# A transformer block in split fp32 on one core: how a VectorE-fed stream starts its products, seven weight tiles side by side

## The chip, the cores and the metric

The kernel runs on one core of a Trainium2 chip. TensorE multiplies (PE in the profile), VectorE (DVE) and ScalarE (ACT) do elementwise work, GpSimd (POOL) some adds and a few DMA issues, SyncE (SP) issues the weight loads. The metric is the device time of one execution in microseconds (us), the median over runs. A measurement of this kernel can tell about 1% from no change, some 22 us.

## What is computed

One block on 272 tokens (16 meta tokens and 256 real ones) of width 2048: half an FFN, a mixer, half an FFN, each between two RMS norms:

```python
h = h + 0.5 * _rmsnorm(_swiglu(_rmsnorm(h, norm_ffn1_pre), ffn1_w_gu, ffn1_w_down), norm_ffn1_post)
m = _hybrid_mixer(_rmsnorm(h, norm_mix_pre), w_in, ..., w_out, cos, sin)
h = h + _rmsnorm(m, norm_mix_post)
h = h + 0.5 * _rmsnorm(_swiglu(_rmsnorm(h, norm_ffn2_pre), ffn2_w_gu, ffn2_w_down), norm_ffn2_post)
return h[:, N_META:]
```

The FFN is `(silu(h @ W_g) * (h @ W_u)) @ W_down` with inner width 5632. The mixer multiplies by `w_in`, runs a multi-scale pooling and a latent attention of 16 heads, gates both, adds them and multiplies by `w_out`. All is fp32.

## The kernel before

**Layout.** Activations lie transposed: 128 partitions by tokens, so the width of 2048 is 16 tiles of the stream (`KD = 16`), each 128 x 272, or 128 x 256 from the mixer's gates on, where the meta tokens are no longer needed. `T` is that width: `L = 272` or `R = 256`. `h` is the residual stream, `h[:, k]` its tile k.

**Split products.** An fp32 product is made of three products of rounded parts, high by high, high by low, low by high (`mm3`, L221 to L225). At width 256 the first two are one matmul of 512 columns into the two halves of a PSUM bank (`mm_wide`, L227 to L231), and `join` adds the halves when the bank is read. Every operand therefore has a high part (a rounded copy) and a low part (the difference).

**Weights.** All weight tiles (128 x 128) stand in DRAM in the order of use, eight to a DMA. Class `Weights` cuts each load into pieces of four tiles (`PT = 4`): ScalarE writes a piece's high part (L93), VectorE subtracts it to make the low part (L102). There are six buffers for pieces (`HL = 6`). `take`, called before each weight tile's matmuls, loads and divides ahead: when piece p is taken, the high parts up to piece p + 4 and the low parts up to p + 3 are queued. Every engine works through its queue in the order in which the program issues it; there is no scheduler that reorders.

**Steps that come later.** `later` keeps a list of small steps with a delay in weight tiles; `take` counts one tick per tile and issues the steps that are due. The reading of banks, the activation and the splitting of results go through it, so that they sit between the weight pieces in the engines' queues.

**The stream.** A stage that begins with a norm doesn't wait for it: the factor of the norm is one number per token, so the products use the unscaled stream times the gain, and the results are scaled by `rs` when they are read. Class `Stream` (L290 to L319) makes the 16 tiles of x one by one. `step(s)` for tile k = s + 1 queues, in this order: the high part of tile k on ScalarE (L304), the update of tile k + 1 (below), the low part of tile k on VectorE (L308), and its square (ScalarE, L280) with the add into `acc` (GpSimd, L283). The update, made in `advance` (L378), finishes the stage before: `t[k] * b` on VectorE (L382; b is the norm's factor, read from PSUM), then the add into `h[k]` (L383), on VectorE for tiles 0 and 1 and on GpSimd for the other 14. After the last tile `scale` sums the squares over partitions on TensorE (`rms_sums`), takes root and reciprocal, and `spread` broadcasts the factor on TensorE (`rms_spread`, L264) and copies it to `rs` on VectorE (L318).

**The wave.** In `products` (L321) a stage with a stream first runs six results side by side, each in a PSUM bank: for each k the stream's step, then one weight tile for each of the six results. The sums come ahead of the products of the last k, the spread behind them. The six banks are read afterwards, one every 12 ticks (`SPACE`). All other results follow one by one over all k, in banks called `m`. There are eight PSUM banks.

**The transition.** `post` (L358) ends a stage: it reads each result, squares it, scales it into `t`, sums the squares (`rms`, L267), with `WARM = (3, 7)` idle matmuls of 128 columns ahead of the spread and behind it. There are three waves with a stream: the first FFN's, whose stream arrives from DRAM (`arrive`), the mixer's first products (transition T1) and the second FFN's (transition T2). The end of the kernel (L776 to L788) multiplies `t` by the last norm's factor, adds `h` and writes the result, on VectorE from b in PSUM and for four of the 16 tiles on GpSimd from a copy in `rs`.

## Time and profile before

| | |
|---|---|
| median of 3 runs | 2237.63 us (2224.92 to 2239.29) |
| the profiled execution | 2238.56 us |
| its span | 2236.8 us |
| PE busy | 2211.0 us, 99% |
| VectorE busy | 1372.7 us, 61% |
| ScalarE busy | 1162.4 us, 52% |
| GpSimd busy | 213.8 us, 10% |
| T1, last down product to the first tile after the wave | 805.09 to 851.98 us |
| T2, the same | 1463.95 to 1508.32 us |
| last norm's factor to the end of the span | 2223.6 to 2236.8 us |

In the lines of the profile L102 is line 102 of the kernel. A group's line has the engine, the operation, output<-input by the program's names, shapes, the count after an x, then the busy time and the mean of one in ns, then the engine's idle time before it and what ended it. A line of the timeline begins with its start from the span's start and its duration, in us; brackets give the idle time before it. A line of the waits has total us, number of times, and the longest. A line of windows has, for each engine, the busy time and the count, then the granted clock, the DMA share and GB/s. Matmuls overlap, so a start-to-start time says what one costs, and a "busy" TensorE may still wait inside.

### The profile page before, as it was taken

The page shows a single profiled execution, that of the slowest core. Times are in us where ns is not written, and L with a number is a line of the kernel's source. Part 1 is how long each engine was busy: PE and PEld are TensorE (multiplying, and loading weights), DVE is VectorE, ACT ScalarE, POOL GpSimd, SP SyncE. Part 2 cuts the span into 40 slices and gives each one's busy share as a digit, 9 for nine tenths or more (in the row PEclk, how much of TensorE's full clock was granted, in tenths as well). Part 3 has the DMA queues.
Part 4 walks back from the last instruction along what each step waited for, and adds up shares of the span by engine and source line. Part 5 has one row for each costly group of instructions (what it writes and reads, how often), then busy time and mean ns, then how long its engine had stood idle before and what let it go on. Part 6 is the DMA issues. An engine that isn't in the chain of part 4 may idle for free.

```text
span 2236.8 us, 39512 instructions
## 1 busy us (share of the span) xinstructions
PE 2211.0 (99%) x15040; PEld 2059.2 (92%) x15040; DVE 1372.7 (61%) x2525; ACT 1162.4 (52%) x2310; POOL 213.8 (10%) x228
## 2 busy tenths in 40 slices
PE   9999999999999999999999999999999999999997
PEld 9999999999999999988899988888888888888886
DVE  6555555555444477766688876587666666655554
ACT  6444444444444454555566655665555555555453
POOL 2000000000000043300132111150000000000001
PEclk9999999999999999999999999999999999999999
DMA  6555555555555545556533355545555555555553
GB/s 232 177 172 175 176 177 170 178 177 174 181 178 169 180 150 171 179 180 196 178 125 133 129 189 191 187 144 192 186 187 185 185 188 188 188 189 180 190 185 124
DMA packets 109311, 393.46 MB, mean 176 GB/s; under 512 B 12288, under 2 KB 13696, under 8 KB 109120
## 3 DMA queue, kind: packets, MB, share of 16 engines
q1 hardware_dynamic: 108576, 389.19, 53.7%
q8 instruction: 118, 1.93, 0.4%
q0 software_dynamic: 400, 1.61, 0.2%
q14 instruction: 73, 0.60, 0.1%
q10 hardware_dynamic: 144, 0.13, 0.0%
HBM read 388.78 MB, written 2.10 MB: 175 GB/s over the span
## 4 chain that ended last, share of the span: by engine, by line
PE 95%; DVE 3%; issue 1%; ACT 0%; DMA 0%; SPq 0%; DVEq 0%; ACTq 0%
PE m L229 30%; PE m L231 15%; PE m L223 13%; PE m L225 13%; PE m L224 13%; DVE lo L102 2%; PE w L229 1%; PE s L665 1%; PE w L231 1%; DVE x L308 1%; PE po L225 1%; PE po L224 1%; PE po L223 1%; PE w L225 1%; PE w L224 1%
## 5 line engine op out<-in xcount | busy, mean ns | idle before, releaser
L102 DVE TENSOR_TENSOR lo<-raw,hi 128x512 fp32r<-128x512 f32 x1472 | 1016.3, 718 | 279.0 <-ACT hi L93 275.2
L93 ACT ACTIVATE hi<-raw 128x512 fp32r<-128x512 f32 x1472 | 894.7, 627 | 448.6 <-PE m L224 279.2
L229 PE MATMUL m<-x,hi 128*128 128x512 f32 x1824 | 643.3, 398 | 0.0
L231 PE MATMUL m<-x,lo 128*128 128x256 f32 x1824 | 512.7, 281 | 0.0
L223 PE MATMUL m<-x,hi 128*128 128x272 f32 (+1 forms) x1488 | 429.4, 289 | 0.0
L225 PE MATMUL m<-x,lo 128*128 128x272 f32 (+1 forms) x1488 | 429.0, 288 | 0.0
L224 PE MATMUL m<-x,hi 128*128 128x272 f32 (+1 forms) x1488 | 428.2, 288 | 0.0
L229 PEld LDWEIGHTS m<-x,hi 128*128 128x128 f32 x1824 | 342.7, 188 | 83.4
L231 PEld LDWEIGHTS m<-x,lo 128*128 128x128 f32 x1824 | 344.6, 189 | 0.0
L224 PEld LDWEIGHTS m<-x,hi 128*128 128x128 f32 x1488 | 282.9, 190 | 0.0
L223 PEld LDWEIGHTS m<-x,hi 128*128 128x128 f32 x1488 | 279.6, 188 | 0.0
L225 PEld LDWEIGHTS m<-x,lo 128*128 128x128 f32 x1488 | 279.5, 188 | 0.0
L283 POOL TENSOR_TENSOR acc<-acc,sq 128x272 f32<-128x272 f32 (+1 forms) x88 | 88.9, 1010 | 1525.7 <-ACT sq L280 1510.5
L229 PE MATMUL m<-a,hi 128*128 128x512 f32 x660 | 233.2, 399 | 0.0
L223 PE MATMUL m<-a,hi 128*128 128x272 f32 (+1 forms) x748 | 215.6, 288 | 0.0
L225 PE MATMUL m<-a,lo 128*128 128x272 f32 (+1 forms) x748 | 215.6, 288 | 0.0
L224 PE MATMUL m<-a,hi 128*128 128x272 f32 (+1 forms) x748 | 215.2, 288 | 0.0
L231 PE MATMUL m<-a,lo 128*128 128x256 f32 x660 | 185.4, 281 | 0.0
L396 DVE TENSOR_TENSOR gu<-m,rs 128x272 f32<-128x272 f32 x82 | 36.2, 442 | 228.5 <-PE m L225 228.5
L229 PEld LDWEIGHTS m<-a,hi 128*128 128x128 f32 x660 | 124.0, 188 | 30.9
L224 PEld LDWEIGHTS m<-a,hi 128*128 128x128 f32 x748 | 142.4, 190 | 0.0
L223 PEld LDWEIGHTS m<-a,hi 128*128 128x128 f32 x748 | 140.7, 188 | 0.0
(214 smaller groups left out, 2723.6 us busy)
## 6 DMA issues: line engine op xcount, KB each, us to landing
raw<-w SPq DMA_DIRECT2D x735, 512.0 KB, 3.6
h<-hT POOLq DMA_DIRECT2D x4, 272.0 KB, 5.4
out<-t SPq DMA_DIRECT2D x8, 128.0 KB, 1.9
out<-t SPq DMA_DIRECT2D x4, 256.0 KB, 2.0
h<-hT SPq DMA_DIRECT2D x1, 544.0 KB, 8.6
raw<-w SPq DMA_DIRECT2D x2, 256.0 KB, 3.5
MA<-tables POOLq DMA_DIRECT2D x1, 480.0 KB, 3.8
h<-hT SPq DMA_DIRECT2D x2, 136.0 KB, 3.5
```

What stands on the lines that cost most here:

```text
L93: nc.scalar.activation(hi, t, AF.Copy)
L102: self.nc.vector.tensor_tensor(lo, t, hi.bitcast(F32), op=ALU.subtract)
L223: mm(o, wh, xh, start=first, stop=False)
L224: mm(o, wh, xl, start=False, stop=False)
L225: mm(o, wl, xh, start=False, stop=last)
L229: mm(b.rearrange("p (b c) -> p b c", b=2), w[0], x.both(k, R), start=first, stop=last, skip_group_check=True)
L231: mm(b[:, :R], w[1], x.hi(k, R), start=False, stop=last, skip_group_check=True)
L283: pool_e.tensor_tensor(acc[:, :T], acc[:, :T], s[:, :T], op=ALU.add)
L308: dve.scalar_tensor_tensor(self.x.lo(k), src, g, hi.bitcast(F32), op0=ALU.mult, op1=ALU.subtract)
L396: scale = lambda src: dve.tensor_tensor(u, src, rs[:, :T], op=ALU.mult)
L665: mm(o, x[:, t], y[:, :n], start=j == 0, stop=j == 4)
```

## The change

1. **The first stream tile of T1 and T2.** In the stage before, three results before its end, ScalarE scales `h[0]` and `t[0]` by the next gain (`old`, `new`). Once the factor b is there, `Stream.begin` makes tile 0 on VectorE alone: `new *= b`, high = `old + new` rounded, `new = old + new`, low = `new` - high. The update of `h[0]` itself, and the squares of tiles 0 and 1, come later, at tile 2.
2. **The order of the first step.** For k = 0 `products.begin` takes all weight tiles and issues for each the two products with the stream's high part; the products with the low part follow for all of them. `Weights.keep` limits the division of pieces meanwhile, so that no buffer still needed is taken.
3. **Seven results side by side** instead of six (`WAVE = 7`) in all three waves. The last of them is read first.
4. **GpSimd's adds in the waves go to VectorE**, those into `h` and those into `acc`, in the first FFN's wave too.
5. **The factor b is copied to SBUF by ScalarE** (`r`), into spare room of `t`'s buffer or, in T1, of the buffer MA, whose allocation and table load move ahead of the first down products. Updates read r, and b's bank is free. At the end of the kernel VectorE and GpSimd both read r.
6. **The sums** come after the third result of the last k, the spread after the sixth.
7. `WARM` is (3, 3).

```diff
-WARM = (3, 7)
-GAP, SPACE = 4, 12
+WARM = (3, 3)
+GAP, SPACE, WAVE = 4, 12, 7
 ...
-        while self.n_split < min(upto, self.total * CH // PT):
+        while self.n_split < min(upto, self.most, self.total * CH // PT):
 ...
+    def keep(self, on):
+        self.most = len(self.order) // PT + HL if on else 1 << 30
 ...
-        pool_e.tensor_tensor(acc[:, :T], acc[:, :T], s[:, :T], op=ALU.add)
+        e.tensor_tensor(acc[:, :T], acc[:, :T], s[:, :T], op=ALU.add)
 ...
+        def begin(self):
+            (old, new, r), hi = self.first, self.x.hi(0)
+            dve.tensor_tensor(new, new, r, op=ALU.mult)
+            dve.tensor_tensor(hi, old, new, op=ALU.add)
+            dve.tensor_tensor(new, old, new, op=ALU.add)
+            dve.tensor_tensor(self.x.lo(0), new, hi.bitcast(F32), op=ALU.subtract)
 
         def step(self, s):
             k, T = s + 1, self.T
+            if k < 0 and self.first:
+                self.begin()
+                return
             todo = self.update(k + 1) if k + 1 < KD else ()
-            if 0 <= k < KD:
+            split = 0 <= k < KD and not (k == 0 and self.first)
+            if split:
                 src, g, hi = h[:, k, L - T :], gain(self.g, k), self.x.hi(k)
                 act(hi, src, AF.Copy, scale=g)
             for f in todo:
                 f()
-            if 0 <= k < KD:
+            if split:
                 dve.scalar_tensor_tensor(self.x.lo(k), src, g, hi.bitcast(F32),
                                          op0=ALU.mult, op1=ALU.subtract)
-                self.last = squares(src, T, k, k == KD - 1)
+            if self.late and k == self.late:
+                for f in self.update(0):
+                    f()
+            if self.late <= k < KD:
+                for j in range(0 if k == self.late else k, k + 1):
+                    self.last = squares(h[:, j, L - T :], T, j, j == KD - 1, dve)
 ...
+        def begin():
+            todo = []
+            W.keep(True)
+            for i in range(wave):
+                w, t = W.take((names[i][0], 0, names[i][1])), T[i] if isinstance(T, list) else T
+                for wi in w:
+                    mm(banks[i][:, :t], wi, x.hi(0, t), start=wi is w[0], stop=False, skip_group_check=wide[i])
+                todo.append((w[0], t))
+            for i, (wh, t) in enumerate(todo):
+                c = R if wide[i] else 0
+                mm(banks[i][:, c : c + t], wh, x.lo(0, t), start=False, stop=False, skip_group_check=wide[i])
+            W.keep(False)
 ...
-                if k == n_k - 1:
-                    spread = stream.scale()
 ...
+            if stream and k == 0:
+                begin()
+                continue
             for i in range(wave):
                 part(i, k, banks[i])
-        if stream:
-            spread()
-        for i in range(wave):
-            later((1 + SPACE * i, lambda i=i: evac(i, banks[i], wide[i])))
+                if stream and k == n_k - 1 and i in (2, 5):
+                    spread = stream.scale() if i == 2 else spread()
+        for j in range(wave):
+            i = (j - 1) % wave if stream else j
+            later((1 + SPACE * j, lambda i=i: evac(i, banks[i], wide[i])))
 ...
+                if j == KD - 3 and g_pre is not None:
+                    for name, src in (("old", h[:, 0, L - T :]), ("new", t[:, 0, :])):
+                        first.append(temp(name)[:, :T])
+                        act(first[-1], src, AF.Copy, scale=gain(g_pre, 0))
 ...
-        return t, rms([acc] + last, T, DM, half, wait)
+        b = rms([acc] + last, T, DM, half, wait)
+        if first:
+            first.append(b[:, :T])
+        act(r, b[:, :T], AF.Copy)
+        return t, r, first
 ...
-            e = pool_e if k > 1 else dve
-            return (lambda: dve.tensor_tensor(t[:, k, :], t[:, k, :], b[:, :T], op=ALU.mult),
-                    lambda: e.tensor_tensor(hk, hk, t[:, k, :], op=ALU.add))
-        return Stream(T, g_pre, update)
+            return (lambda: dve.tensor_tensor(t[:, k, :], t[:, k, :], r, op=ALU.mult),
+                    lambda: dve.tensor_tensor(hk, hk, t[:, k, :], op=ALU.add))
+        return Stream(T, g_pre, update, first)
 ...
-        products(names, KD, x.x, T, 6, evac, x)
+        products(names, KD, x.x, T, WAVE, evac, x)
 ...
-        o, f = t[:, a : a + n, :], (b if e is dve else rs)[:, :R]
+        o = t[:, a : a + n, :]
+        f = r[:, None, :].to_broadcast([P, n, R]) if n > 1 else r[:, None, :]
         e.tensor_tensor(o, o, f, op=ALU.mult)
         e.tensor_tensor(o, o, h[:, a : a + n, NMETA:], op=ALU.add)
         nc.sync.dma_start(out[:, a : a + n, :], o)
-        if a == 0:
-            act(rs[:, :R], b[:, :R], AF.Copy)
```

More of the change, by code (lines that the diff above doesn't have):

```diff
@@ L72, in __init__ @@
         self.n_loaded = self.n_split = self.n_low = 0
+        self.most = 1 << 30
     def load(self, upto):
@@ L272, in rms, with squares @@
         return b
-    def squares(src, T, j, last=False):
+    def squares(src, T, j, last=False, e=pool_e):
         if j == 0:
@@ L290, in build, with __init__ @@
     class Stream:
-        def __init__(self, T, g, update):
-            self.T, self.g, self.update = T, g, update
+        def __init__(self, T, g, update, first=None):
+            self.T, self.g, self.update, self.first = T, g, update, first
             self.x = Two(KD, T, "x")
             self.last = []
+            self.late = 2 if first else 0
+        def begin(self):
[4 more added lines that the diff above has]
+            dve.tensor_tensor(self.x.lo(0), new, hi.bitcast(F32), op=ALU.subtract)
         def step(self, s):
             k, T = s + 1, self.T
+            if k < 0 and self.first:
+                self.begin()
+                return
             todo = self.update(k + 1) if k + 1 < KD else ()
-            if 0 <= k < KD:
+            split = 0 <= k < KD and not (k == 0 and self.first)
+            if split:
                 src, g, hi = h[:, k, L - T :], gain(self.g, k), self.x.hi(k)
@@ L355, in products, with post @@
             evac(i, b, wide[i])
-    def post(names, n_k, x, T, g_post, half, wave, wait):
-        t = slot3(KD, T, F32, "t")
-        last = []
+    def post(names, n_k, x, T, g_post, half, wait, g_pre, wave, spare=None):
+        room = slot(SLOT, F32, "t")
+        t = room[:, : KD * T].rearrange("p (a b) -> p a b", a=KD)
+        r = room[:, KD * T : KD * T + T] if T == R else spare()
+        last, first = [], []
         def evac(j, b, wide):
@@ L409, in evac @@
                   (GAP, lambda: dve.tensor_tensor(lo, u, hi.bitcast(F32), op=ALU.subtract)))
-        products(names, KD, x.x, T, 6, evac, x)
+        products(names, KD, x.x, T, WAVE, evac, x)
         later.flush()
         load_table()
-        return post([(w_down, j) for j in range(KD)], KF, a, T, g_post, True, 0, wait)
+        return post([(w_down, j) for j in range(KD)], KF, a, T, g_post, True, wait, g_pre, 0, spare)
     warm(10, zero)
@@ L423, in arrive, with spare @@
                 lambda: pool_e.dma_start(h[:, k + 4 : k + 6, :], hT[:, k + 4 : k + 6, :]),)
-    t, b = ffn(Stream(L, G_F1PRE, arrive), "ffn1_w_gu", "ffn1_w_down", G_F1POST, WARM)
-    x = advance(t, b, L, G_MPRE)
-    MA = slot(SLOT, F32, "MA")
-    pool_e.dma_start(MA[:, :C_KPE], tables_d)
+    made = {}
+    def spare():
+        made["MA"] = slot(SLOT, F32, "MA")
+        pool_e.dma_start(made["MA"][:, :C_KPE], tables_d)
+        return made["MA"][:, SLOT - L :]
+    after = ffn(Stream(L, G_F1PRE, arrive), "ffn1_w_gu", "ffn1_w_down", G_F1POST, WARM, G_MPRE, spare)
+    x = advance(*after, L, G_MPRE)
+    MA = made["MA"]
     cos, sin, mask = MA[:, C_COS:C_SIN], MA[:, C_SIN:C_MASK], MA[:, C_MASK:C_KPE]
@@ L521, in evac_in @@
             windows(i - 9)
-    products(names, KD, x.x, width, 6, evac_in, x)
+    products(names, KD, x.x, width, WAVE, evac_in, x)
     zp_rest = slot(SLOT, F32, "zp")
@@ L772, in build @@
     load_table()
-    t, b = post([("w_out", m) for m in range(KD)], KD, y, R, G_MPOST, False, 6, WARM)
-    t, b = ffn(advance(t, b, R, G_F2PRE), "ffn2_w_gu", "ffn2_w_down", G_F2POST, (0, 0))
+    after = post([("w_out", m) for m in range(KD)], KD, y, R, G_MPOST, False, WARM, G_F2PRE, 6)
+    t, r, _ = ffn(advance(*after, R, G_F2PRE), "ffn2_w_gu", "ffn2_w_down", G_F2POST, (0, 0), None)
     for a, n, e in ((0, 1, dve), (1, 1, dve), (3, 1, pool_e), (2, 1, dve), (4, 2, dve), (8, 1, pool_e), (6, 2, dve),
                     (9, 2, dve), (11, 1, pool_e), (12, 2, dve), (15, 1, pool_e), (14, 1, dve)):
-        o, f = t[:, a : a + n, :], (b if e is dve else rs)[:, :R]
-        if n > 1:
-            f = f[:, None, :].to_broadcast([P, n, R])
-        else:
-            f = f[:, None, :]
+        o = t[:, a : a + n, :]
+        f = r[:, None, :].to_broadcast([P, n, R]) if n > 1 else r[:, None, :]
         e.tensor_tensor(o, o, f, op=ALU.mult)
```

4 lines of the change are left out of this document (2 added, 2 removed).

## The prediction

> **What bounds the kernel now.** I read the page first, then the waits of the two transitions, then their timelines, then the tail.
>
> ```profile
> span 2236.8 us, 39512 instructions
> PE 2211.0 (99%) x15040; PEld 2059.2 (92%) x15040; DVE 1372.7 (61%) x2525; ACT 1162.4 (52%) x2310; POOL 213.8 (10%) x228
> ```
> ```profile
> 700.00:800.00 100.00, 100.00 (x799) 100.00 (x798) 44.87 (x67) 44.78 (x79) 5.16 (x7) 1.00 0.56 181
> 2100.00:2200.00 100.00, 100.00 (x568) 86.69 (x567) 51.13 (x78) 49.23 (x89) 5.75 (x6) 1.00 0.59 189
> ```
>
> TensorE sets the time. In an undisturbed stretch (second fence, busy time by window) it issues 799 matmuls in 100 us, 0.125 us each: a weight tile at width 272 costs three, 0.376 us. In the narrow half 568 are 284 pairs, 0.352 us per tile. The diff leaves the tile count alone, so it can only win what TensorE loses elsewhere: at the transition into the mixer (T1) and into the second FFN (T2). There one engine holds it:
>
> ```profile
> PE w L224 <- DVE x L308: 2.8, 6, 0.5
> PE w L229 <- DVE x L308: 3.7, 7, 0.7
> ```
>
> TensorE waits for VectorE's low part of the next stream tile, in T1 (L224) and T2 (L229). Why VectorE is late stands in the groups of T1's wave (812 to 846 us) beside the weight differences of a quiet stretch (600 to 700 us, last row):
>
> ```profile
> L102 DVE TENSOR_TENSOR lo<-raw,hi 128x512 fp32r<-128x512 f32 x21 | 25.9, 1259 | 0.0
> L283 POOL TENSOR_TENSOR acc<-acc,sq 128x272 f32<-128x272 f32 x13 | 15.9, 1223 | 0.0
> L383 POOL TENSOR_TENSOR h<-h,t 128x272 f32<-128x272 f32 x13 | 12.6, 967 | 6.8 <-DVE t L382 6.8
> L102 DVE TENSOR_TENSOR lo<-raw,hi 128x512 fp32r<-128x512 f32 x67 | 45.4, 692 | 55.6 <-ACT hi L93 55.6
> ```
>
> The weight difference takes 1.259 us beside GpSimd's adds and 0.692 us without: 21 x 0.567 = 11.9 us lost to 26 GpSimd adds, 0.46 us per add. VectorE's idle time there is 0.0.
>
> The timeline of T1, from the last down product to the first tile after the wave:
>
> ```profile
> 805.09 0.72 PE L253 MATMUL rms<-const,acc 128*128 128x1 f32 x6
> ...
> 808.07 0.44 DVE L382 TENSOR_TENSOR t<-t,rms 128x272 f32<-128x272 f32 x1 [0.93 <-PE rms L264]
> 808.54 0.44 DVE L383 TENSOR_TENSOR h<-h,t 128x272 f32<-128x272 f32 x1
> 808.90 0.43 DVE L382 TENSOR_TENSOR t<-t,rms 128x272 f32<-128x272 f32 x1
> 809.02 0.52 ACT L304 ACTIVATE x<-h,gains 128x272 fp32r<-128x272 f32 x1 [2.09 <-DVE h L383]
> 809.59 0.39 PE L223 MATMUL w<-x,hi 128*128 128x272 f32 x1
> 809.73 0.50 DVE L308 SCALAR_TENSOR_TENSOR x<-h,gains,x 128x272 fp32r<-128x272 f32 x1
> 810.14 0.43 DVE L382 TENSOR_TENSOR t<-t,rms 128x272 f32<-128x272 f32 x1
> 810.27 0.41 ACT L280 ACTIVATE sq<-h 128x272 f32<-128x272 f32 x1
> 810.28 0.40 PE L224 MATMUL w<-x,hi 128*128 128x272 f32 x1 [0.29 <-DVE x L308]
> ...
> 847.58 1.28 DVE L102 TENSOR_TENSOR lo<-raw,hi 128x512 fp32r<-128x512 f32 x2
> ...
> 847.82 0.72 PE L253 MATMUL rms<-const,acc 128*128 128x1 f32 x6
> ...
> 849.07 0.37 PE L223 MATMUL w<-x,hi 128*128 128x272 f32 x1
> ...
> 851.40 0.73 PE L264 MATMUL rms<-const,sd 128*128 128x128 f32 x6
> ...
> 851.98 0.36 PE L223 MATMUL m<-x,hi 128*128 128x256 f32 x1
> 852.17 0.44 DVE L318 COPY rs<-rms 128x272 f32<-128x272 f32 x1 [1.83 <-PE rms L264]
> ```
>
> T1 lasts 851.98 - 805.09 = 46.89 us; its 96 tiles need 36.06 us. The loss is 10.8 us. T2 in the same view:
>
> ```profile
> 1463.95 0.50 PE L253 MATMUL rms<-const,acc 128*128 128x1 f32 x4
> ...
> 1466.55 0.42 DVE L382 TENSOR_TENSOR t<-t,rms 128x256 f32<-128x256 f32 x1 [0.80 <-PE rms L264]
> 1467.00 0.42 DVE L383 TENSOR_TENSOR h<-h,t 128x256 f32<-128x256 f32 x1
> ...
> 1468.76 0.47 PE L229 MATMUL w<-x,hi 128*128 128x512 f32 x1 [0.69 <-DVE x L308]
> ...
> 1508.32 0.48 PE L229 MATMUL m<-x,hi 128*128 128x512 f32 x1
> ```
>
> 44.37 us less 96 x 0.352 = 33.79: 10.6 us lost. Both together are 21.4 us, under 1% (22.4 us): even a perfect transition would stay within it.
>
> **The start of the wave.** Now: multiply, add, ScalarE's high part, TensorE at 809.59, then a wait for the low part to 810.28; without it the second matmul would have come 0.125 us after the first, so the wave effectively starts at 810.16. After: VectorE multiplies the pre-scaled `new` by r (808.07), writes the high part itself (808.54 to 808.98), and TensorE starts some 0.05 us later, as it now does behind ScalarE: 809.03. The low part (809.37 to 809.81) is covered by 14 matmuls that need only the high part, 1.75 us. **T1 gains 1.1 us.** T2, whose wide matmul waits for both parts, starts at 1467.00 + 0.42 + 0.06 = 1467.48 instead of 1468.76: **1.3 us**. The pre-scaling is two ScalarE copies two tiles before the end of the stage before, beside matmuls: nothing. The four warm-up matmuls fewer lay in TensorE's idle time: nothing. If r's copy on ScalarE (about 0.4 us) were late, it would hold only tile 1's multiply at 809.73; it is done by about 808.5.
>
> **VectorE's queue in the wave.** Without GpSimd its weight differences go back to a spacing of 0.60 us (1.28 for two, of which the last takes its whole 0.69). Per stream tile, by the rows' start-to-start times: multiply 0.47, add 0.36, low part 0.41, and the moved square add, like the add, 0.36. With seven tiles, 1.75 weight differences, 1.05. Sum 2.65 us against TensorE's 7 x 0.376 = 2.63. In T2, 16 columns fewer, I estimate 0.45 + 0.35 + 0.40 + 0.35 + 1.05 = 2.60 against 7 x 0.352 = 2.46. An add with two SBUF inputs (L383) costs 0.44, as a multiply from PSUM does, so I charge nothing for reading r from SBUF; a square add is unlikely to be under 0.3 or over 0.5.
>
> **The pile at the third tile.** I walk T1's queue. After the low part: multiply and add of tiles 1 and 2 from 809.73, low part 1 at 811.39, done 811.89. TensorE wants it at 809.03 + 2.63 + 0.125 = 811.79: 0.1 us lost. Two weight differences to 813.0, tile 3's update to 813.8, low part 2 done at 814.33; TensorE wants it at about 814.5: in time. Now the deferred update of tile 0 (0.83), and the square adds of tiles 1 and 2, the first of which waits for two squares on ScalarE (0.41 us each, issued some 0.32 apart, so about 0.8 us). Behind these stand two weight differences, tile 4's update and low part 3: 814.24 + 0.91 + 0.81 + 0.72 + 1.20 + 0.83 + 0.50 = 819.21. TensorE wants it at 817.15: **2.1 us lost**. From there T1's queues run level: 12 x 0.02 lost, less 0.83 because the last tile brings no update, so nothing. T2 loses 0.3 at tile 1, 2.2 at the pile by the same walk, and 12 x 0.14 - 0.8 = 0.8 later, 3.3 in all.
>
> **The end of the wave.** Seven banks and the sums' bank are all eight, so the next tile must wait for VectorE's copy out of the latter. From the spread's first matmul to the copy's end is 852.61 - 851.40 = 1.21 us; TensorE has 0.58 of spread and one tile of 0.38. **0.3 us lost** in each of three waves, 0 to 0.9 as VectorE is free or in a weight difference. The sums themselves, and the spread, are the same work in both.
>
> The sums (849.07 - 847.82 = 1.25 us) and the spread (0.58) stay. So T1's loss goes from 10.8 to (809.03 - 805.09) + 2.2 + 0.3 + 1.83 = 8.3 us: **gain 2.5**. T2's sums and spread have two thirds of the matmuls, 1.2 us by estimate; its loss goes from 10.6 to (1467.48 - 1463.95) + 3.3 + 0.3 + 1.2 = 8.3: **gain 2.3**.
>
> **The first wave pays.** Its pieces arrive one by one:
>
> ```profile
> 8.28 0.39 PE L223 MATMUL w<-x,hi 128*128 128x272 f32 x1 [0.28 <-ACT hi L93]
> 9.14 0.39 PE L225 MATMUL w<-x,lo 128*128 128x272 f32 x1 [0.35 <-DVE lo L102]
> ```
>
> By 9.27 TensorE has done all 15 matmuls of five tiles. With the low products last it has done eight of piece 0 and two of tile 4; the other five come later: 0.6 us, plus the bank, **0.9 us lost**.
>
> **The tail pays.** The result's multiplies read r from SBUF, after ScalarE's copy:
>
> ```profile
> 2223.61 0.42 DVE L784 TENSOR_TENSOR t<-t,rms 128x256 f32<-128x256 f32 x1 [0.80 <-PE rms L264]
> 2224.07 0.38 ACT L788 ACTIVATE rs<-rms 128x256 f32<-128x256 f32 x1 [1.46 <-DVE t L784]
> ...
> 2228.36 1.18 DVE L785 TENSOR_TENSOR t<-t,h 128x512 f32<-128x512 f32 x1
> ```
>
> The copy moves to the front of the path: 0.44 us with its handover. And GpSimd's eight operations stay here, where VectorE's multiplies so far escaped them. An add of two tiles takes 1.18 us against the 0.692 of the same form in the quiet stretch: 0.49 lost. Eight GpSimd operations by 0.46 are 3.7 us, of which two pairs, 1.0, are paid already: at most 2.7 more, at least 0. I take 2.3, near the top, because every VectorE operation now has two SBUF inputs. **2.7 us lost.** The Trainium skill (SBUF — State Buffer, the section on the two separate sides) has the pair of ports that VectorE and GpSimd share as an exclusive lock for a whole instruction. It is the rule that speaks against this edit; a full block would make the loss per GpSimd operation its own length, and the tail's loss, by my estimate, some 2 us larger. The two rows, with 0.49 lost, agree with the conflict, not with that size.
>
> **The sum.** 2.5 + 2.3 - 0.9 - 2.7 = 1.2 us gained. The profiled execution took 2238.56 us (span 2236.8); the median, 2237.63, is 0.9 below. 2238.56 - 1.2 - 0.9 = 2236.5 us: no change that can be told.
>
> **Rivals.** (1) VectorE becomes the bound of both waves, and the kernel gets slower. If weight differences come singly, at 0.69 instead of 0.60, a tile costs 2.81 us in T1 and 2.76 in T2, against 2.63 and 2.46: 12 x 0.18 - 0.8 = 1.3 us more in T1 and 12 x 0.16 = 1.9 more in T2, so 2239.7 us. It decides from about 2.7 us per tile on. For it: 2.65 against 2.63 is no reserve. Against it: with a full queue the differences come in pairs at 0.60. Chance 0.2.
>
> (2) The pile costs nothing, because prefetched pieces and earlier squares shorten it: 4.3 us more gained, 2232.2 us. For it: over the whole wave VectorE's sum is level with TensorE's. Against it: its queue is in order. Chance 0.2.
>
> (3) The stall at the pile drops TensorE's clock. In this trace one long wait does so (the wait, then windows whose column before the last two is the granted clock):
>
> ```profile
> 1119.97 0.45 PE L665 MATMUL s<-VP,att 128*128 128x144 f32 x2 [2.15 <-DVE att L625]
> ```
> ```profile
> 1120.00:1122.00 2.00, 2.00 (x13) 2.00 (x14) 1.89 (x8) 0.81 (x2) 0.00 (x0) 0.73 0.02 4
> 1122.00:1124.00 2.00, 2.00 (x11) 2.00 (x11) 1.48 (x7) 1.31 (x6) 0.00 (x0) 0.50 0.22 33
> 1124.00:1126.00 2.00, 2.00 (x17) 2.00 (x17) 0.87 (x3) 1.12 (x4) 1.71 (x2) 0.91 0.59 229
> ```
>
> After a wait of 2.15 us the clock is 0.73, 0.50, 0.91: 0.54 + 1.00 + 0.18 = 1.7 us lost. At both piles: 3.4 us, 2239.9 us. Against it: low part 2, the last piece and low part 3 split the stall, so that its longest piece is about 1.5 us. The Trainium skill (TensorE: Matmul & The Clock Gate, Part 1) puts the drop behind about 3.4 us of idling; with these rows the clock fell after less continuous idling than that. Chance 0.1.
>
> **The numbers.** The forecast has 0.5, the rivals 0.2, 0.2 and 0.1. Its own bounds: the tail between 0.4 and 3.1 us lost, the bank between 0 and 2.7 over three waves, the square add (28 of them, 0.06 under to 0.14 over) between 1.7 gained and 3.9 lost: 2231 to 2242. The shown runs of the kernel before include 2224.92 beside 2237.63 and 2239.29, a spread larger than anything this change does by my sum; the time after can fall there as well, some 2 us lower. So the range is 2223 to 2242. About 1% is what a measurement of this kernel can tell from no change. No case reaches 22 us: faster 0.02, same 0.96, slower 0.02.
>
> **What would show it.** In the profile after: the weight difference of L102 in both waves at about 0.69 instead of 1.26 us; no GpSimd add there; the first matmul of T1's wave some 3.9 us after the last down product, T2's 3.5; the longest wait of each wave at its fourth tile, on a low part, about 2 us; multiplies of two tiles in the tail at over 1 us instead of 0.68, and its first multiply 0.44 us behind ScalarE's copy. The prediction is wrong if VectorE still has no idle time in T1's wave while TensorE waits at every tile (rival 1), if no wait of a microsecond is left (rival 2), or if the clock falls below 1.00 there (rival 3); and by size, if a transition loses under 6 or over 10 us beyond its tiles.

## The result: 0.7% slower, all of it outside the transitions

The changed kernel takes 2245.77 us (median of 12 runs, 2233.32 to 2247.65), the kernel before 2226.01 us (median of 12 runs beside it, 2222.59 to 2239.29). The ratio is 1.0066, with a 95% interval of 1.0045 to 1.0086; it goes by all the runs and so isn't the quotient of the two medians. That matters here, since the times of the kernel before lie in two groups, seven of these twelve between 2222.6 and 2226.1 and five between 2237.6 and 2239.3; the mean granted clock doesn't tell the groups apart, it is 0.996 to 0.998 in both wherever a run of that kernel beside the experiments has it on record. A ratio therefore depends on how many of the runs beside it fall into each group, here and below. Eleven of the twelve after lie between 2244.6 and 2247.7, one at 2233.32. The predicted 2236.5 us, and its range up to 2242, miss it. The difference is under the 1% that a measurement of this kernel can tell from no change; what follows goes by the traces.

The profiled execution after took 2244.69 us, 6.1 us more than the one before (2238.56), and its span is 6.1 us longer too. The head of its page:

```profile
span 2242.9 us, 39445 instructions
...
PE 2213.4 (99%) x15031; PEld 2061.9 (92%) x15031; DVE 1369.7 (61%) x2601; ACT 1166.2 (52%) x2314; POOL 141.2 (6%) x158
```

TensorE is still the engine that sets the time. Its waits after (total us, times, longest):

```profile
...
PE w L363 <- ACT hi L94: 1.9, 2, 1.5
PE w L363 <- DVE x L309: 1.6, 2, 0.8
PE w L234 <- DVE x L326: 1.4, 1, 1.4
PE w L229 <- DVE x L326: 1.3, 1, 1.3
...
PE w L230 <- DVE lo L107: 0.5, 1, 0.5
PE w L236 <- DVE lo L107: 0.5, 1, 0.5
...
PE m L234 <- DVE rs L341: 0.2, 1, 0.2
```

The 13 waits on VectorE's low parts in the waves (6.5 us before) are gone. In their place stand one at the pile of each transition (L229 and L234, with 0.5 us on a weight's low part just ahead), one at the start of each (L363 on L309), and one that was not looked for: 1.5 us on ScalarE's first weight part, L94. The last row is the bank wait; it is small here and matters later. The timeline after, first wave, T1, T2 and tail:

```profile
1.32 2.31 POOL L473 DMA_DIRECT2D h<-hT  x4 [0.45 <-issue]
...
6.68 0.63 ACT L94 ACTIVATE hi<-raw 128x512 fp32r<-128x512 f32 x1 [1.72 <-DMA raw<-w]
...
7.36 0.59 PE L363 MATMUL w<-x,hi 128*128 128x272 f32 x1 [1.52 <-ACT hi L94]
...
8.48 0.43 PE L363 MATMUL w<-x,hi 128*128 128x272 f32 x1
8.70 0.43 PE L363 MATMUL w<-x,lo 128*128 128x272 f32 x1
...
58.06 0.39 PE L228 MATMUL m<-x,hi 128*128 128x272 f32 x1
...
811.50 0.72 PE L258 MATMUL rms<-const,acc 128*128 128x1 f32 x6
...
814.47 0.40 ACT L426 ACTIVATE MA<-rms 128x272 f32<-128x272 f32 x1 [1.14 <-PE rms L269]
814.98 0.44 DVE L308 TENSOR_TENSOR new<-new,rms 128x272 f32<-128x272 f32 x1 [1.43 <-ACT MA L426]
...
815.95 0.39 PE L363 MATMUL w<-x,hi 128*128 128x272 f32 x1 [0.74 <-DVE x L309]
...
863.12 0.38 PE L228 MATMUL m<-x,hi 128*128 128x256 f32 x1
...
1467.96 0.50 PE L258 MATMUL rms<-const,acc 128*128 128x1 f32 x4
...
1472.01 0.36 PE L363 MATMUL w<-x,hi 128*128 128x256 f32 x1 [0.81 <-DVE x L309]
...
1517.22 0.50 PE L234 MATMUL m<-x,hi 128*128 128x512 f32 x1 [0.17 <-DVE rs L341]
...
2226.13 0.71 PE L269 MATMUL rms<-const,sd 128*128 128x128 f32 x4 [0.55 <-DVE sd L263]
2226.88 0.38 ACT L426 ACTIVATE t<-rms 128x256 f32<-128x256 f32 x1 [1.00 <-PE rms L269]
2227.29 0.43 DVE L837 TENSOR_TENSOR t<-t 128x256 f32<-128x256 f32 x1 [1.22 <-ACT t L426]
...
2231.96 1.21 DVE L837 TENSOR_TENSOR t<-t 128x512 f32<-128x512 f32 x1
...
2239.18 0.42 DVE L838 TENSOR_TENSOR t<-t,h 128x256 f32<-128x256 f32 x1
```

And the first wave of the kernel before:

```profile
5.07 0.63 ACT L93 ACTIVATE hi<-raw 128x512 fp32r<-128x512 f32 x1 [0.29 <-DMA raw<-w]
...
11.38 0.71 POOL L423 DMA_DIRECT2D h<-hT  x1
...
24.64 0.56 POOL L423 DMA_DIRECT2D h<-hT  x1
...
45.65 0.37 PE L223 MATMUL m<-x,hi 128*128 128x272 f32 x1
```

Between the same two points of both kernels, less the 16 weight tiles that a seventh result brings into a wave (3 x 0.125 us each at 272 columns; 3 x 0.12 in T1, whose seventh result is 256 wide; 0.352 in T2), the 6.1 us are:

| stretch | before | after | less tiles | change |
|---|---|---|---|---|
| start to first tile after the first wave | 45.65 | 58.06 | 6.02 | +6.4 |
| T1, last down product to first tile after the wave | 46.89 | 51.62 | 5.76 | -1.0 |
| from there to T2 | 611.97 | 604.84 | -5.76 | -1.4 |
| T2, as T1 | 44.37 | 49.26 | 5.63 | -0.7 |
| second FFN, to the last norm's spread | 714.54 | 708.91 | -5.63 | 0.0 |
| tail, from that spread to the end | 13.94 | 16.77 | | +2.8 |

So the loss lies in the first wave and the tail, the two places that were not the aim. The stretch from the first wave to T1 is level: 759.44 us before, 753.44 + 6.02 after.

### The profile page after: what moved, and what is told of

Same layout as the page of the kernel before. It is cut to its first block, busy times and chain, and to the rows that moved or that the text cites. A ratio compares the mean times of both kernels' runs of the same rounds, so it can differ in the third digit from the quotient of the medians.

```text
span 2242.9 us, 39445 instructions
## 1 busy us (share of the span) xinstructions
PE 2213.4 (99%) x15031; PEld 2061.9 (92%) x15031; DVE 1369.7 (61%) x2601; ACT 1166.2 (52%) x2314; POOL 141.2 (6%) x158
## 4 chain that ended last, share of the span: by engine, by line
PE 98%; DVE 1%; ACT 0%; DMA 0%; issue 0%; SPq 0%; ACTq 0%; DVEq 0%
PE m L234 29%; PE m L236 15%; PE m L228 12%; PE m L230 12%; PE m L229 12%; PE w L234 2%; PE w L236 1%; PE w L229 1%; PE w L230 1%; PE w L228 1%; PE s L721 1%; PE po L230 1%; PE po L229 1%; PE po L228 1%; PE k L230 0%; PE k L229 0%
## 5 line engine op out<-in xcount | busy, mean ns | idle before, releaser
L107 DVE TENSOR_TENSOR lo<-raw,hi 128x512 fp32r<-128x512 f32 x1472 | 986.8, 699 | 282.3 <-ACT hi L94 278.4
L94 ACT ACTIVATE hi<-raw 128x512 fp32r<-128x512 f32 x1472 | 896.1, 628 | 448.3 <-PE m L229 274.7
L234 PE MATMUL m<-x,hi 128*128 128x512 f32 x1808 | 637.7, 398 | 0.2 <-DVE rs L341 0.2
L228 PE MATMUL m<-x,hi 128*128 128x272 f32 (+1 forms) x1456 | 420.3, 289 | 0.1
L230 PE MATMUL m<-x,lo 128*128 128x272 f32 (+1 forms) x1456 | 419.8, 288 | 0.0
L229 PE MATMUL m<-x,hi 128*128 128x272 f32 (+1 forms) x1456 | 419.1, 288 | 0.0
L234 PEld LDWEIGHTS m<-x,hi 128*128 128x128 f32 x1808 | 339.7, 188 | 82.7 <-DVE rs L341 0.5
L236 PEld LDWEIGHTS m<-x,lo 128*128 128x128 f32 x1808 | 341.6, 189 | 0.0
L229 PEld LDWEIGHTS m<-x,hi 128*128 128x128 f32 x1456 | 276.8, 190 | 0.0
L228 PEld LDWEIGHTS m<-x,hi 128*128 128x128 f32 x1456 | 273.6, 188 | 0.6 <-DVE rs L341 0.6
L230 PEld LDWEIGHTS m<-x,lo 128*128 128x128 f32 x1456 | 273.5, 188 | 0.0
L234 PE MATMUL m<-a,hi 128*128 128x512 f32 x660 | 233.2, 399 | 0.0
L229 PE MATMUL m<-a,hi 128*128 128x272 f32 (+1 forms) x748 | 215.2, 288 | 0.0
L234 PEld LDWEIGHTS m<-a,hi 128*128 128x128 f32 x660 | 124.0, 188 | 31.0
L229 PEld LDWEIGHTS m<-a,hi 128*128 128x128 f32 x748 | 142.3, 190 | 0.0
L230 PEld LDWEIGHTS m<-a,lo 128*128 128x128 f32 x748 | 140.7, 188 | 0.0
```

What stands on the lines that cost most here:

```text
L94: nc.scalar.activation(hi, t, AF.Copy)
L107: self.nc.vector.tensor_tensor(lo, t, hi.bitcast(F32), op=ALU.subtract)
L228: mm(o, wh, xh, start=first, stop=False)
L229: mm(o, wh, xl, start=False, stop=False)
L230: mm(o, wl, xh, start=False, stop=last)
L234: mm(b.rearrange("p (b c) -> p b c", b=2), w[0], x.both(k, R), start=first, stop=last, skip_group_check=True)
```

## The experiments

### The first wave: who sends GpSimd's loads

In the kernel before, GpSimd's queue held, in order, the adds of the squares and the four loads of `hT` by which `arrive` brings tiles 8 to 15. Each load had to wait for an add, and went out at 11.38 us or later. With the adds on VectorE nothing stands ahead of the loads: all four go out at 1.32 us, 1.1 MB beside the first weights. The theory: this delays the first weights, and with them TensorE. Its rivals are VectorE's queue, which now has the square adds, and the new order of the first step. The changed kernel, with the first wave's adds back on GpSimd:

```diff
-                    self.last = squares(h[:, j, L - T :], T, j, j == KD - 1, dve)
+                    self.last = squares(h[:, j, L - T :], T, j, j == KD - 1, dve if self.first else pool_e)
```

> The changed kernel with one edit: in the first wave alone the square adds go back to GpSimd, so that its queue again holds the four later stream loads back behind them. Theory A (GpSimd's loads start at 1.3 us because nothing is queued ahead of them, crowd out the first weights and stream tiles, and TensorE's clock drops behind the wait): the first load on GpSimd's queue starts past 10 us, the first product at about 5.8 us, its steps are 0.125 us, and the first tile after the wave starts at about 52 to 53 us instead of 58.06; the span falls by 5 to 6 us to about 2237. Rival B (seven tiles side by side with the low products last cost the first wave): the first tile after the wave stays at 57 us or later. Rival C (VectorE's square adds cost it): the time is recovered as with A, so that this run alone does not tell A from C.

Measured: 2239.15 us (2237.63 to 2240.95), ratio to before 1.0048 (1.0026 to 1.0071), 6.6 us under the changed kernel. Its timeline:

```profile
4.96 0.61 ACT L94 ACTIVATE hi<-raw 128x512 fp32r<-128x512 f32 x1
...
12.07 0.71 POOL L473 DMA_DIRECT2D h<-hT  x1
...
52.50 0.39 PE L228 MATMUL m<-x,hi 128*128 128x272 f32 x1
```

The first weight part is back from 6.68 to 4.96 us, and the first tile after the wave from 58.06 to 52.50: 5.6 of the 6.4 us. What is left, 52.50 - 45.65 - 6.02 = 0.8 us, is the cost of the new order that the prediction had put at 0.9.

The next run leaves the adds on VectorE and moves the loads to ScalarE's queue, where they stand behind other work:

```diff
-                lambda: pool_e.dma_start(h[:, k + 4 : k + 6, :], hT[:, k + 4 : k + 6, :]),)
+                lambda: nc.scalar.dma_start(h[:, k + 4 : k + 6, :], hT[:, k + 4 : k + 6, :]),)
```

> The changed kernel with one edit: the four later stream loads are issued from ScalarE's queue instead of GpSimd's, in their place in the program; the square adds stay on VectorE. Theory A: ScalarE's queue holds them back as GpSimd's did in the kernel before, so the first tile after the wave starts at about 52 to 54 us and the span falls by 4 to 6 us. Rival B and rival C: 57 us or later, since order, width and square adds are as in the changed kernel.

Measured: 2241.94 us (2238.41 to 2245.16), ratio 1.0070 (1.0051 to 1.0088).

```profile
11.77 0.45 ACTq L473 DMA_DIRECT2D h<-hT  x1
...
53.48 0.39 PE L228 MATMUL m<-x,hi 128*128 128x272 f32 x1
```

With VectorE's queue as in the changed kernel, 4.6 of the 5.6 us are back once the loads go out late. VectorE's adds can account for the other 1.0 at most. The span fell by only 2.7 us (2242.9 to 2240.2), less than the 4 to 6 expected. In this trace, unlike the changed kernel's, the granted clock also falls behind the pile of each transition, where TensorE waits for the fourth tile (the wait of T1, then the window behind it: TensorE's busy time and matmuls, granted clock, DMA share, GB/s):

```profile
821.95 0.40 PE L229 MATMUL w<-x,hi 128*128 128x272 f32 x1 [1.30 <-DVE x L326]
```
```profile
822.00:824.00 2.00, 2.00 (x10) 0.61 0.48 174
```

The next 2 us read 0.54, and behind T2's pile the 4 us from 1480 read 0.65. T1 takes 52.45 us here, 51.62 in the changed kernel; T2 takes 49.18 and 49.26. And the counterpart, the kernel before with its first wave's adds on VectorE and nothing else changed:

```diff
...
-                self.last = squares(src, T, k, k == KD - 1)
+                self.last = squares(src, T, k, k == KD - 1, dve if self.g == G_F1PRE else pool_e)
```

> The kernel before with one edit: in the first wave the square adds go to VectorE, so that nothing is queued ahead of GpSimd's four loads. Six tiles side by side, old order. Theory A: the loads start at about 1.3 us, the first product at about 7.4 us instead of 5.75, and the first tile after the wave starts 4 to 6 us later than 45.65; the span rises from 2236.8 to about 2242. Rival B: no change, within 1 us.

Measured: 2229.55 us (2225.28 to 2241.82), ratio 1.0013 (0.9986 to 1.0041): the ratio settles nothing, since this kernel too has two groups of times. Group against group, its seven lower runs have a median of 2228.64 us against 2224.10 for the 24 lower runs of the kernel before beside it; its three upper ones 2240.05 against 2238.91. Its timeline shows where:

```profile
1.32 2.29 POOL L423 DMA_DIRECT2D h<-hT  x4 [0.45 <-issue]
...
49.72 0.37 PE L223 MATMUL m<-x,hi 128*128 128x272 f32 x1
```

The loads go out at 1.32 us, and the first tile after the wave comes at 49.72 in place of 45.65: the one edit costs 4.1 us there, in a kernel without any of the other changes.

How a late first weight can become 5.6 us: first the landing. The pages' rows of the first two weight loads, before and after:

```profile
raw<-w SPq DMA_DIRECT2D x2, 256.0 KB, 3.5
```

```profile
raw<-w SPq DMA_DIRECT2D x2, 256.0 KB, 5.2
```

The Trainium skill (Trainium Kernel Development and Optimization, Key Constraints) says that loads issued from the queues of SyncE, ScalarE and GpSimd share the same 16 DMA engines and interleave there; the two rows, 1.7 us apart, agree. Then the clock. The windows of the changed kernel with early sums (below), whose first wave begins with the same program, have the granted clock in the column before the last two, and ahead of it TensorE's busy time and matmuls:

```profile
10.00:12.00 2.00, 1.28 (x4) 0.50 1.05 402
12.00:14.00 2.00, 2.00 (x11) 0.50 1.04 415
14.00:16.00 2.00, 2.00 (x10) 0.50 1.02 398
16.00:18.00 2.00, 2.00 (x14) 0.80 1.03 404
```

Its timeline has the two waits at the drop:

```profile
7.40 0.39 PE L363 MATMUL w<-x,hi 128*128 128x272 f32 x1 [1.56 <-ACT hi L94]
...
10.59 0.60 PE L363 MATMUL w<-x,hi 128*128 128x272 f32 x1 [1.32 <-ACT hi L94]
```

After the first of these waits, and within the second, the clock falls; it is at half for 6 us and at 0.80 for 2: 3.0 + 0.4 = 3.4 us lost, twice the late landing itself. The Trainium skill (TensorE: Matmul & The Clock Gate, Part 1) gives the drop one idle window of about 3.4 us; here the idling was in two pieces shorter than that, with eight products between.

In the changed kernel's own trace the first clock record stands at 16.94 us, and the column reads 1.00 where there is none, so only the steps tell. The products stand 0.22 us apart (8.48 and 8.70 above) up to 16.76 us, where 0.125 is full speed, and the idle matmuls ahead of them 0.21 us apart to the last, against 0.11 at the end of those of the kernel before: by these steps the clock had not yet risen there. That late weights and a half clock belong together is read from the traces, no run shows it alone. All five kernels whose loads go out early (first product at 7.05 to 7.40 us) have 6.8 us or more of half clock in the first wave; of the nine other traces (5.50 to 5.93 us) one has, that of the mended kernel below.

### The tail

The changed kernel with the tail as it was: VectorE multiplies from PSUM, and the copy for GpSimd follows the first multiply.

```diff
+        if g_pre is None:
+            return t, (b, r), first
         act(r, b[:, :T], AF.Copy)
...
+    b, r = r
...
-        o = t[:, a : a + n, :]
-        f = r[:, None, :].to_broadcast([P, n, R]) if n > 1 else r[:, None, :]
+        o, f = t[:, a : a + n, :], (b[:, :R] if e is dve else r)
...
+        if a == 0:
+            act(r, b[:, :R], AF.Copy)
```

> The changed kernel with one edit: the last norm's factor is read as in the kernel before, by VectorE from PSUM, with the copy for GpSimd behind VectorE's first multiply. Theory: from the last norm's spread to the last add takes 2.9 us less than in the changed kernel, where it is 13.0 us (2226.13 to 2239.18), so about 10.2 us; the span falls by about 2.9 us. Rival (the tail's loss is only the copy at its front): 0.5 us less.

Measured: 2241.69 us (2239.45 to 2243.47), ratio 1.0065 (1.0043 to 1.0088), 4.1 us under the changed kernel.

```profile
2223.71 0.71 PE L269 MATMUL rms<-const,sd 128*128 128x128 f32 x4 [0.55 <-DVE sd L263]
...
2233.89 0.42 DVE L841 TENSOR_TENSOR t<-t,h 128x256 f32<-128x256 f32 x1
```

From the spread to the last add it takes 10.18 us, in the changed kernel 2239.18 - 2226.13 = 13.05. The edit is worth 2.9 us in the trace; that its median is 4.1 lower I can't put down to it, since in its trace the first wave too ends 0.9 us earlier (57.16 us), and the stretch between T1 and T2 is 1.5 us shorter (603.33 against 604.84): from 1126 to 1130 us, behind a wait of 2.1 us in the attention that both traces have, the granted clock is 0.57 in the changed kernel and 1.00 here.

### Two cadences of the wide products

The profiled executions of the changed kernel and of the first, second and fourth of these runs took between 0.9 us less and 6.1 us more than the one of the kernel before, which is of its upper group; their medians stand 15 to 21 us above its lower group. The windows show where two groups of times can come from. Of 1700 to 1800 us, in the middle of the second FFN, the rows of before and after (window, TensorE's busy time and count, granted clock, DMA share, GB/s):

```profile
1700.00:1800.00 100.00, 100.00 (x568) 1.00 0.57 186
```

```profile
1400.00:1450.00 50.00, 50.00 (x290) 1.00 0.57 185
1700.00:1800.00 100.00, 100.00 (x569) 1.00 0.56 185
```

The after's first row, in the products of `w_out`, has 290 matmuls in 50 us; in the FFN there are 284.5. Both at full granted clock, with no wait of TensorE. The profiled kernel before has 285 in `w_out` too, and its products of `w_out` take 90.44 us against 88.95: that accounts for the -1.4 us in the table's third row. So the pairs of a 512-column and a 256-column matmul run in one of two cadences, 0.352 us a pair (100 / 284) or 0.345 (50 / 145), both a little low since a window also counts the matmuls that it cuts. A trace keeps one of them through the whole second FFN. Over the 707 us of the FFN that is 707 x (1 - 568/579) = 13 us. The prediction's 0.352 us a tile is the slower one. Three more profiles of the kernel before:

> The kernel before, unchanged, for its profile: its times lie around 2224 and around 2238 us, its profile at hand is of the second sort. Theory D (a step of the steady products is slower in the one than in the other): in an execution near 2224 us the windows of 100 us of the first FFN hold some 0.6% more matmuls than the 799 of the profile at hand. Rival E (one wait or one clock drop of 13 us in one place): the windows hold the same, and one stage is 13 us shorter.

> The same kernel once more, as above, so that one profile of each sort is likelier.

> The kernel before once more, unchanged, for its profile alone. If the two times of this kernel (about 2224 and 2238 us) are the two cadences of its wide products, a profiled execution near 2224 shows some 289 matmuls in 50 us over the whole second FFN, and one near 2238 shows 285, with nothing else that differs by more than 1 or 2 us; the rival (something else makes its two times) has the same count in both.

Measured: 2239.01, 2237.11 and 2236.01 us, each in the slow cadence through the second FFN (567 to 569 matmuls in 100 us). No profiled execution fell near 2224, so that the kernel before runs in the quick cadence there is inferred from the size alone: its groups lie some 13 us apart.

What sets the cadence? The changed kernel has seven banks in use and waits 0.17 us for the eighth at the entry of the second FFN's remaining tiles (its last row of the waits). With six results side by side a bank is free:

```diff
-GAP, SPACE, WAVE = 4, 12, 7
+GAP, SPACE, WAVE = 4, 12, 6
...
-            i = (j - 1) % wave if stream else j
+            i = (j - 1) % wave if stream and wave % 2 else j
```

> The changed kernel with six tiles side by side (the banks read in their old order), all else as in the change. Theory: VectorE needs 1.60 + 1.5 x 0.60 = 2.50 us per tile in the mixer's wave against TensorE's 2.24, so it becomes the bound there: that wave loses some 12 x 0.26 = 3 us more than with seven; in the second FFN's 2.45 against 2.11, some 4 us more. The first wave still has the early loads. In all 5 to 7 us slower than the changed kernel. Rival (the width is what costs): the kernel falls back to about 2225 us.

Measured: 2237.48 us (2236.36 to 2239.72), ratio 1.0023 (1.0001 to 1.0044), where 5 to 7 us more than the changed kernel had been expected.

```profile
1700.00:1800.00 100.00, 100.00 (x579) 1.00 0.58 190
```

The quick cadence, and 8.3 us less than the changed kernel. Six results cost something: 13 us of cadence should have given 2232.7, so about 5 us are lost, the size that was expected, in longer waits for the stream (L326: 8 in T1, 3.1 us, and 8 in T2, 4.6, against 1.3 and 1.4). What the expectation hadn't is the cadence. Next, seven results again, with the other losses that the traces had shown mended: the first wave's adds on GpSimd, the tail as before, the copy of the factor behind the first multiply that needs it, and tile 0's deferred update and square moved from tile 2's step to the last:

```diff
...
-            dve.tensor_tensor(new, new, r, op=ALU.mult)
+            dve.tensor_tensor(new, new, b, op=ALU.mult)
+            copy()
...
-            if self.late and k == self.late:
-                for f in self.update(0):
-                    f()
...
+            elif 1 <= k < KD:
+                self.last = squares(h[:, k, L - T :], T, k - 1, k == KD - 1, dve)
+                if k == KD - 1:
+                    for f in self.update(0):
+                        f()
+                    self.last += squares(h[:, 0, L - T :], T, 1, True)
```

> The changed kernel with four mends: square adds of the first wave back on GpSimd; the tail as in the kernel before; ScalarE's copy of the factor behind VectorE's first multiply; the update of tile 0 and its square behind the last low part, as a third source of the sums, instead of at tile 2. Theory: against the changed kernel's profile (2242.9) the first wave gains 6, the tail 2.9, the copy 0.5 in each transition, the pile 2 in each: a span of about 2229, and no wait of over 0.6 us on a low part in either transition. Rival (the stall at the fourth tile comes from too slow a VectorE and not from the pile): the stalls stay, spread over the wave, and the span is about 2233.

Measured: 2233.66 us (2231.79 to 2236.57), ratio 1.0009 (0.9987 to 1.0030), 12.1 us under the changed kernel. Its waits have no row on the stream's low part (here L327) any more, so the pile is gone, and the start waits for 0.7 us in all instead of 1.6. Its span is 2234.2 us where about 2229 had been expected: the first wave ends at 54.92 us, 2.4 later than in the first run, with products 0.227 us apart up to 14.05 us, and the products of `w_out` too are in the slow cadence (285 in 50 us). The second FFN is still in the slow one, 569 in 100 us, and the bank wait is still there. In its timeline the last product of the second FFN is followed by the sums at 2218.27:

```profile
1511.22 0.50 PE L234 MATMUL m<-x,hi 128*128 128x512 f32 x1 [0.17 <-DVE rs L345]
...
2218.27 0.50 PE L258 MATMUL rms<-const,acc 128*128 128x1 f32 x4
```

From its first tile after the wave to there are 707.05 us; in the changed kernel, by its trace, 2224.27 - 1517.22 = 707.05 as well. The next two runs put this wait away in the same way, by taking the sums after the first result of the last k and the spread after the fourth, so that VectorE has read the sums' bank before the wave ends. First in the mended kernel:

```diff
-                if stream and k == n_k - 1 and i in (2, 5):
-                    spread = stream.scale() if i == 2 else spread()
+                if stream and k == n_k - 1 and i in (0, 3):
+                    spread = stream.scale() if i == 0 else spread()
```

> e7 with one thing changed: in each seven-wide wave the sums' matmuls come after the first tile's last low product (instead of the third) and the spread's after the fourth (instead of the sixth), so that VectorE's copy out of the sums' bank is over before the next tile needs that bank. Theory (the 0.2 us bank wait at the entry of a stage sets the two wide products running in their slower cadence, some 285 matmuls in 50 us instead of 288.5): no wait of the first tile after the wave on the copy of rs, the second FFN's products at 288 to 289 matmuls in 50 us, and with that some 13 us less than e7's 2233.7: 2220 to 2222 us. Rival (the cadence comes from something else, seven tiles side by side for one): the wait is gone, the cadence is still near 285, and the time is within 1 us of e7's: 2233 to 2234 us.

Measured: 2220.02 us (2217.04 to 2220.96), ratio 0.9938 (0.9917 to 0.9958), 13.6 us under the mended kernel.

```profile
1504.74 0.42 DVE L345 COPY rs<-rms 128x256 f32<-128x256 f32 x1 [0.54 <-PE rms L269]
1505.58 0.40 PE L234 MATMUL m<-x,hi 128*128 128x512 f32 x1
...
2199.49 0.28 PE L258 MATMUL rms<-const,acc 128*128 128x1 f32 x2
```

The copy ends at 1505.16, the first product follows at 1505.58 without a wait, and the stretch takes 693.91 us: 13.1 less for the same matmuls. Then in the changed kernel itself, the same two lines and nothing else:

> The changed kernel with one thing changed: the sums after the first tile's last low product and the spread after the fourth (as in e8), all its other losses (first wave, tail, pile, copy of r) left in. Theory (the wait of the first tile on the copy of rs sets the slow cadence): that wait is gone, some 289 matmuls in 50 us in the second FFN, and 13 us less than the changed kernel's 2245.8: 2231 to 2234 us. Rival (in e8 the mending of the pile had its part in the cadence): the wait is gone, still near 285 matmuls in 50 us, and 2244 to 2246 us. Sums that come early can also wait for the last square of the stream, up to 1 us a wave, which would add up to 3 us to either.

Measured: 2231.31 us (2230.09 to 2233.12), ratio 1.0018 (0.9999 to 1.0037), 14.5 us under the changed kernel, 579 matmuls in 100 us. All other losses are still in it (its waits have the pile, 1.3 and 1.4 us, and 2.9 us on L94), and the cadence alone turned. The mending of the pile had no part in that. Last, the mended kernel with six results, whose sums come late and which has a free bank:

> e7 with six tiles side by side in place of seven, the banks in the old order: the first wave's squares on GpSimd, the tail as before, the copy of r behind the first multiply, the deferred update and its square behind the last low part. Theory (a bank that is free at the entry of a stage, as with any six-wide wave, gives the faster cadence): 288 to 289 matmuls in 50 us in the second FFN, and 2237.5 (six wide alone) less 6 for the first wave, 3 for the tail, 1 for the copies and 3 to 4 for the pile: 2223 to 2226 us. Rival (the squares' place in the first wave or the tail, not the bank, decides the cadence): near 285 matmuls in 50 us and 2236 to 2239 us.

Measured: 2225.08 us (2221.74 to 2226.97), ratio 0.9975 (0.9951 to 0.9999), 579 matmuls in 100 us. So late sums alone don't bring the slow cadence, and seven results alone don't: all five seven-wide kernels with the wait (the changed one, those with the adds back, the loads on ScalarE or the tail back, and the mended one) have it in their traces, and the two without the wait have not. The other times fit: the ten runs of each of these last kernels without the wait (six results alone, six results mended, and both with early sums) lie within 5.3 us of each other, with no second group 13 us away. What stays together in these runs is the wait and the place of the sums and the spread: the two early-sums runs move both at once, and in their traces the quick steps begin already behind the spread, three tiles before the entry where the wait was. So the two lines turn the cadence; that it is the wait in them is likely, not shown. The stretch of the second FFN has just two lengths in all traces, 707.05 or 693.9 us with seven results, 712.7 or 699.5 with six.

## Why the prediction was wrong

The steps in the transitions were mostly right; most of what failed lies outside them.

**"The first wave pays", 0.9 us: the term that failed, 6.4 us measured.** What it costed, the new order, is right: 0.8 us (the first run). It left out that the adds that move to VectorE leave a queue in which loads stood behind them. The prediction counted the adds' cost on the engine that receives them, and nothing on the one that loses them. GpSimd's four rows of `hT` loads were in the trace of before, at 11.38 to 24.64 us, spaced by work and not by the DMA; that row was the one to ask about.

**How the terms add up to the miss of 9.3 us (2245.77 against 2236.5).** The first wave adds 5.5 us to the forecast, T1 1.5, T2 1.6 and the tail 0.1; the products of `w_out`, which the profiled execution after had in the quick cadence, take 1.4 off. That is 7.3 us between the two profiled executions. The forecast also took 0.9 us off for the median, and the profiled execution after lies 1.1 under its own.

**The two cadences: not in the sum, and the reason why the medians lie 19.8 us apart.** The forecast was worked out from an execution in the slow cadence, and the changed kernel stayed in it, so the cadence of the second FFN is no part of those 9.3 us. But of the 19.8 us some 13 are that the kernel before runs in either cadence, as its two groups of times suggest, and the changed one, as far as its runs and traces show, nearly always in the slow one. Its run at 2233.32 would be the quick one by its size; no trace shows it. The spread 2224.92 to 2239.29 was seen, and called larger than anything that the change does, but it was taken as something that no edit would set. The bank wait itself was foreseen, at 0.3 us a wave; measured are 0.2 us once, and the edit that ends it is worth 13.

**The starts, 1.1 and 1.3 us gained: failed by the copy.** The first product was to come 3.9 and 3.5 us after the last down product; it came after 815.95 - 811.50 = 4.45 and 1472.01 - 1467.96 = 4.05. The prediction let the multiply and ScalarE's copy run side by side ("If r's copy on ScalarE (about 0.4 us) were late, it would hold only tile 1's multiply at 809.73"). The trace has the first multiply behind the copy, at 814.98, released by it. With the copy second, in the mended kernel, T1's start takes 812.37 - 808.36 = 4.01 us.

**The pile, 2.1 and 2.2 us: right.** One wait at the fourth tile of each wave, 1.3 and 1.4 us on its low part, with 0.5 on a weight's low part just ahead: 1.8 and 1.9. Rival 2 (it costs nothing) falls. The moved deferred update and squares took it away.

**The weight differences back at 0.69 us: right.** In T1's wave after they take 684 ns each. Rival 1 (VectorE the bound) falls: the low parts wait nowhere else in the waves.

**The transitions, 2.5 and 2.3 us gained: 1.0 and 0.7.** The starts take 0.5 each of the difference. The sum was also out by its tiles: it took T1's 96 tiles at 0.376, though 16 of them are 256 wide, and 0.352 for T2 is one of two cadences. The remaining microsecond of each lies in single steps of 0.2 us and more in place of 0.125, that I can't put down to a wait.

**Rival 3, the clock drop: not in the changed kernel's trace, but not ruled out.** Its piles drop nothing (33 matmuls in the 4 us behind T1's, at 1.00). With the loads on ScalarE the same waits of 1.3 and 1.4 us are followed by the half clock in both transitions, at a cost of 0.8 us in T1 and none in T2 where the rival had 1.7 for each; the three other traces with these piles have none. The prediction priced the drop by one wait, of 2.15 us in the attention; that wait stands in all 14 traces, and the drop behind it in nine. The first wave, where the half clock cost most, isn't in the rival.

**"The tail pays", 2.7 us: right.** 2.9 us by the two traces, with the first multiply 0.41 us behind the start of the copy and multiplies of two tiles at 1.21 us beside GpSimd.

## What to carry to other kernels

Before an operation is moved off an engine, list what stands behind it in that engine's queue: an add can be what holds four loads back, and taking it away can cost more than the add. When the times of a kernel fall into two groups, count TensorE's instructions per window in each trace before any sum is made: here two lines at the entry of a long stage, beside a wait of 0.17 us, were worth 13 us. Compare group with group: with these lines and the other losses mended the change takes 2220.02 us, 0.9938 of the kernel before, but much of that is the slow group among the runs beside it; under the lower group (2223.0 to 2226.0, median 2224.4) it is 4 us, 0.2%.

## What was not expected of the hardware

The same stream of matmul pairs runs at 0.352 or 0.345 us a pair at a granted clock of 1.00, for 690 us, and which of the two can hang on the order of a few matmuls, with 0.17 us of wait, at its start. What holds it there no run shows. The wait is not the only way into the slow cadence: the kernel before has none there and was slow in all its traces, and in the products of `w_out` four traces of that one kernel have 285 matmuls in 50 us twice and 290 twice.

In the changed kernel with early sums the granted clock fell to half at 10 us, within the second of two waits of 1.56 and 1.32 us, and stayed there for 6 us although TensorE was busy from 12 us on. Whether a wait drops the clock differs between executions: the attention's wait of 2.1 us did in nine of 14 traces, the piles' waits of 1.3 and 1.4 us in one of five.
